# A 16-sublayer network on one core: conv's last normalisation in single blocks, a 64-byte scratch tile, and modulation portions from the eighth block on

## The chip, the cores and the metric

The kernel runs on one core of a Trainium2 chip as one launch. The metric is device time in microseconds (us) from start to end of an execution, lower is better. A profiled execution also gives a span, from the first instruction to the last, and a trace of every instruction. Engines: PE is TensorE (matrix products; PEld its weight loads), DVE is VectorE, ACT is ScalarE, POOL is GpSimd, SP is SyncE, which issues the loads here.

## What is computed

Three blocks follow one another on 256 tokens of width 1024: two layers each, with 16 sublayers in all. The change touches the conv sublayer of the first block, the masks of hgrn, and the feed-forwards in which the second block's modulation is prepared.

```python
def swiglu_ffn(x, w_in, w_out):
    gate, up = jnp.split(x @ w_in, 2, axis=-1)
    return (jax.nn.silu(gate) * up) @ w_out

def conformer_conv_module(x, w_in, b_in, w_dw, b_dw, ln_g, ln_b, w_out, b_out):
    a, gate = jnp.split(x @ w_in + b_in, 2, axis=-1)
    h = a * jax.nn.sigmoid(gate)
    h = lax.conv_general_dilated(h, w_dw[:, None, :], window_strides=(1,),
        padding=[(CONV_WIDTH - 1, 0)], ..., feature_group_count=D_MODEL) + b_dw
    h = jax.nn.silu(layer_norm(h, ln_g, ln_b))
    return h @ w_out + b_out

def second_block(...):
    cond = jax.nn.silu(c)
    for i in range(DEPTH):
        mod = cond @ ada_w[i] + ada_b[i]
        sh0, sc0, g0, sh1, sc1, g1, sh2, sc2, g2 = jnp.split(mod, N_MOD, axis=-1)
        h = modulate(rmsnorm(x, pre_norm[i, 0]), sh0, sc0)
        ...
```

## The kernel before

**Stages.** In order of time: f00, conv, f01, f10, hgrn, f11 (first block; f is a feed-forward), g00, dsa, g01, g10, diff, g11 (second; g is a modulated feed-forward), pool, m0, moba, m1 (third). conv lies at about 211 to 331 us, g00 at 1071 to 1246, g01 at 1363 to 1550.

**Weights.** Every weight matrix comes in chunks of 1 MB (`raw`, three buffers) through SP's queue, in order. ACT rounds a chunk to the matmul's fp32r type in four pieces (`hi`, L330), DVE forms the rest (`lo`, L334), and a product is made of three matmuls: hi by hi, lo by hi, hi by lo. There are five buffers of each, so these conversions run ahead of TensorE until the buffers are full.

**Order.** A scheduler sets the order of instructions on each engine from the order of the code and its dependences; buffers of a pool rotate by name. Each engine then runs its own list in order and waits by semaphores. `issue` (L624) lets code be written in at a given product of a sequence. `finish` (L657) does a sublayer's output product for token halves m = 0 and 1 and, ten products before the end of m = 1, has the next sublayer's transposes of the first half (`split_t`, L502) issued.

**Modulation portions.** The matrix of `ada_w` is worked off in portions of 128 outputs during feed-forwards that don't need it yet: a load of 512 KB (`adaw`, L1176, three buffers) and a multiply with a sum on DVE (`adaj`, L1186). f00, f01, f10 and f11 have 18 each, g00, g01 and g10 24 each, 144 in all. `more()` in `ffn` is called as weight chunks are taken, and does that share of the portions that has come due.

**conv.** Eight blocks of 128 channels: blocks 0 to 2 are convolved on DVE, blocks 3 to 7 on TensorE by `taps`, each in two parts of 16 matmuls on phase copies `ph` (L928). Results go to `y`; `mean` (L905), then the variance (`var`, L959) by one-column matmuls; `rest` (L956, L961) brings the last block's share; `r` is the reciprocal root by POOL, `rb` (L973) spreads it. Then `y` is normalised by groups of two blocks (L978, L979), SiLU on ACT (L983), rounded (L985) and its rest formed (L986). The output product starts with the bias (L990) and goes through L644.

**Scratch.** `prime` (L431) runs a one-column activation of a function that is needed soon, so that ACT loads its table early. Its tile is the first of the pool `tiny`.

Of the kernel before, what the change touches and what calls it, by code (L numbers as in the profile page):

```python
# [11 lines left out]
F32 = mybir.dt.float32  # L12
# [4 lines left out]
AF = mybir.ActivationFunctionType  # L17
# [4 lines left out]
S = 256  # L22
# [270 lines left out]
class _K:  # L293
# [137 lines left out]
    def prime(self, func, after):  # L431

        n = after.shape[0]
        t = self.tiny.tile([128, 1], F32, name="prime", bufs=1)
        self.nc.scalar.activation(t[:n], after, func, scale=0.0)

    def square(self, src, st, n):
# [286 lines left out]
    def ffn(self, s, act):  # L724
        nc, tc = self.nc, self.tc
        nf = 22
        with tc.tile_pool(name="hp_" + s, bufs=2) as hp:
            groups = {}
            jobs = self.ada_jobs.get(s, [])
            if jobs:  # L730
                self.ada_open(hp, jobs)
            takes = [0]

            def more():
                if jobs:
                    takes[0] += 1
                    with tc.issue_after(self.normed_last.ins):
                        self.ada_steps(min(len(jobs), -(-len(jobs) * takes[0] // 24)))

            def hidden(f, p):  # L740
                g, b = divmod(f, 2)
                if b == 0:
                    groups[g] = (hp.tile([128, 2, 256], F32R, name="hh", bufs=4), hp.tile([128, 2, 256], F32R, name="hl", bufs=4))
                hh, hl = groups[g]
                ragged = s[0] == "g" and f == nf - 1
                if ragged:

                    for t in (hh, hl):
                        nc.gpsimd.memset(t[64:, b].bitcast(F32), 0.0)
                n = 64 if ragged else 128  # L750
                sg = hp.tile([128, 256], F32, name="sg")
                h = hp.tile([128, 256], F32, name="h")
                self.added(sg[:n], p[0], slice(0, n))
                nc.scalar.activation(sg[:n], sg[:n], AF.Silu)
                self.added(h[:n], p[-1], slice(128 - n, 128))
                nc.vector.tensor_tensor(h[:n], sg[:n], h[:n], op=OP.mult)
                nc.scalar.activation(hh[:n, b], h[:n], AF.Copy)
                nc.vector.tensor_tensor(hl[:n, b], h[:n], hh[:n, b].bitcast(F32), op=OP.subtract)

            def hs(g):  # L760
                hh, hl = groups[g]
                return [(hh[:, b], hl[:, b]) for b in range(2)]

            p4 = self.first(s, ((0, 1), (2, 3)), act)
            hts = []
            for f in range(4):
                sg = hp.tile([128, 2, 128], F32, name="sg")
                if f % 2 == 0:
                    ht = hp.tile([128, 2, 2, 128], F32, name="hh" if f == 0 else "hl", bufs=4)
                h = ht[:, f % 2]  # L770
                for m in range(2):
                    pp = p4[f][m]
                    nc.scalar.activation(sg[:, m], pp[:, :128], AF.Silu)
                    nc.vector.tensor_tensor(h[:, m], sg[:, m], pp[:, 128:], op=OP.mult)
                hts.append(h)

            def turn():
                for g in range(2):
                    p = self.ps(("tr", "ps")[g])
                    for b in range(2):  # L780
                        for m in range(2):
                            nc.tensor.transpose(p[:, 256 * b + 128 * m:256 * b + 128 * m + 128], hts[2 * g + b][:, m], self.ident)
                    groups[g] = self.split(p, hp)

            self.rows_ahead(s)
            acc = None
            for g in range(2, 11):
                for f in (2 * g, 2 * g + 1):
                    w = self.take(("U", s, f))
                    if f > 4:  # L790
                        more()
                    p = [self.ps(t) for t in (("ps",) if s[0] == "g" and f == nf - 1 else ("ps", "tr"))]
                    products = self.wide_products(w, p)
                    if f == 4:
                        self.issue(products, 26, turn)
                    else:
                        self.issue(products)
                    hidden(f, p)
                    if f == 5:
                        acc = self.new_acc()  # L800
                    for j in ((0, 1) if f == 5 else (g - 1,) if f % 2 and g < 8 else ()):
                        w = self.take(("V", s, j))
                        more()
                        for m in range(2):
                            self.down(m, acc[m], w, hs(j), (128, 128), j == 0, False)
            if jobs:
                self.ada_close()
                self.rows_ahead(s, True)
            held = [(self.take(("V", s, g), g - 7), hs(g), (128, 128)) for g in (7, 8, 9, 10)]
            return self.finish(acc, held, self.cur_post)  # L810
# [58 lines left out]
    def conv(self, act):  # L869
        nc, tc = self.nc, self.tc  # L870
        with tc.tile_pool(name="cv", bufs=2) as cp:
# [18 lines left out]
            ones = cp.tile([128, 128], F32R, name="ones", bufs=1)  # L890
            nc.scalar.activation(ones, pick[:, :128], AF.Copy)
            bias = cp.tile([128, D], F32R, name="bias", bufs=1)
            nc.scalar.activation(bias, brow, AF.Copy)
            nc.vector.tensor_tensor(bias[32:33], brow[32:33], bias[32:33].bitcast(F32), op=OP.subtract)
            self.rows_ahead("conv")

            mean = self.ps("a2")
# [19 lines left out]
            for j in range(DVE_BLOCKS, 8):  # L917
# [5 lines left out]
                for i in range(2):  # L923
                    w = cp.tile([128, 16, 128], F32, name="taps", bufs=3)
                    nc.sync.dma_start(w.rearrange("p d c -> p (d c)"), self.a["ctaps"][2 * (j - DVE_BLOCKS) + i])
                    gv = g[64 * i:64 * i + 64].rearrange("p (t a) -> p a t", a=2)
                    for a in range(2):
                        nc.scalar.activation(x[64 * a:64 * a + 64, i, 15:], gv[:, a], AF.Copy)  # L928
                    for d in range(16):
                        nc.tensor.matmul(pc[:, i], lhsT=w[:, d], rhs=x[:, i, d:d + S // 2], start=(d == 0), stop=(d == 15))  # L930
                    yv = y[64 * i:64 * i + 64, j].rearrange("p (t a) -> p a t", a=2)
                    for a in range(2):
                        h = slice(64 * a, 64 * a + 64)
                        nc.scalar.activation(yv[:, a], pc[h, i], AF.Identity, bias=self.col("bph", 2 * j + i)[h])
                if j < 7:
                    summed(j)
                self.split_ahead(2)
                n = self.TAPS_BEHIND[j - DVE_BLOCKS]
                for at in left[:n]:
# [3 lines left out]
                left = left[n:]  # L943
            self.prime(AF.Silu, sg[:, :1])

            var = [self.ps("a3"), self.ps()]
            rest = self.ps("a0")
            for b in ((0, 1), (2, 3), (4, 5), (6,), (7,)):
                n = len(b)
                yb = y[:, b[0]:b[0] + n]  # L950
# [16 lines left out]
            nc.gpsimd.tensor_tensor(r, v, self.mhalf[:, :2], op=OP.pow)  # L967

            dg = cp.tile([128, 2, 128], F32, name="sg")
            rb = self.ps("a1")  # L970
            for m in range(2):
                nc.vector.tensor_scalar(dg[:, m], self.ident, r[:, m:m + 1], float(D), op0=OP.mult, op1=OP.mult)
                nc.tensor.matmul(rb[:, 128 * m:128 * m + 128], lhsT=means[:, 0], rhs=dg[:, m], start=True, stop=True)  # L973
            oact = self.new_act()
            for g in range(4):
                yg = y[:, 2 * g:2 * g + 2]
                for b in range(2):
                    nc.vector.tensor_tensor(yg[:, b], yg[:, b], rest[:, :S], op=OP.subtract)  # L978
                nc.vector.tensor_tensor(yg, yg, rb[:, None, :S].to_broadcast([128, 2, S]), op=OP.mult)  # L979
                z = cp.tile([128, 2, S], F32, name="sq")  # L980
                for b in range(2):
                    j = 2 * g + b
                    nc.scalar.activation(z[:, b], yg[:, b], AF.Silu, bias=self.col("lnb", j), scale=self.col("lng", j))  # L983
                h = oact[0][:, 2 * g:2 * g + 2]
                nc.scalar.activation(h, z, AF.Copy)  # L985
                nc.vector.tensor_tensor(oact[1][:, 2 * g:2 * g + 2], z, h.bitcast(F32), op=OP.subtract)  # L986
            acc = self.new_acc()
            for m in range(2):
                for n in range(2):
# [5 lines left out]
    def hgrn(self, act):  # L995
        nc, tc = self.nc, self.tc
        with tc.tile_pool(name="hg", bufs=2) as ho, ExitStack() as es:
# [75 lines left out]
            p4 = self.first("hgrn", _U_ORDER["hgrn"][:2], act)  # L1073
            mi = self.tmp.tile([128, D], I32, name="xn", bufs=1)
            nc.sync.dma_start(mi[:, :448], self.a["k_masks"])
            nc.vector.tensor_copy(masks.rearrange("p l t -> p (l t)"), mi[:, :448])
            self.rows_ahead("hgrn")
            for j in range(4):
                pf, pq = ([self.turned(p4[2 * j + i]) for i in range(2)] if j < 2 else
                          [self.proj_u(self.take(("U", "hgrn", 2 * j + i)), act) for i in range(2)])  # L1080
                vals = elems(j, pf, pq)
                for lev in range(8):
                    scores(j, *vals, lev)
            for n, s in enumerate(self.HALVES):
# [777 lines left out]
```

## Time and profile before

| | us |
|---|---|
| median of 3 runs | 2610.27 |
| lowest and highest | 2608.87, 2611.88 |
| profiled execution | 2617.61 |
| its span | 2615.1 |
| PE busy | 2570.5 (98%) |
| DVE busy | 1953.7 (75%) |
| ACT busy | 1504.6 (58%) |

The profiled execution is one of its own; its time lies 7.3 us above the median, so its rows are good for durations and waits, and differences are carried to the median. Its mean granted clock of TensorE is 0.995 of full speed.

### The profile page before, as it was taken

How to read it: one execution, taken by the hardware profiler on the slowest of the kernel's cores; microseconds unless marked ns; L12 is line 12 of the kernel's file. 1: busy time of each engine (PE TensorE's matmuls, PEld its weight loads, DVE VectorE, ACT ScalarE, POOL GpSimd, SP SyncE). 2: the span in 40 equal slices, each digit the busy share in tenths (PEclk: the TensorE clock that was granted, in tenths of full speed). 3: DMA queues.
4: the chain of work that ended last, by engine and by line, in shares of the span. 5: the costliest groups of instructions: out<-in, count | busy, mean ns of one | idle time of the engine just before them, and what ended most of it. 6: DMA issues, size and time to landing. Idle time of an engine off the chain costs nothing.

```text
span 2615.1 us, 37057 instructions
## 1 busy us (share of the span) xinstructions
PE 2570.5 (98%) x13302; PEld 2153.1 (82%) x13302; DVE 1953.7 (75%) x4175; ACT 1504.6 (58%) x3373; POOL 72.4 (3%) x158
## 2 busy tenths in 40 slices
PE   8999999999999999999999999999999999999999
PEld 7888888888888888888778888877788788877887
DVE  7868587687668886886969779777866866677664
ACT  5655455555644555655765565575655655566553
POOL 0000000000000000000000000000100000000000
PEclk9999899999999999999999999999999999999999
DMA  8847376486424675684448668653555545542552
GB/s 326 304 164 282 145 274 233 159 333 228 176 82 178 256 291 188 259 330 181 177 153 324 241 235 330 232 212 129 209 187 184 188 161 199 187 171 97 193 182 92
DMA packets 92711, 554.14 MB, mean 212 GB/s; under 512 B 10716, under 2 KB 11756, under 8 KB 38384
## 3 DMA queue, kind: packets, MB, share of 16 engines
q1 hardware_dynamic: 92528, 551.79, 57.3%
q8 instruction: 104, 1.70, 0.3%
q14 instruction: 79, 0.65, 0.1%
HBM read 550.62 MB, written 1.13 MB: 211 GB/s over the span
## 4 chain that ended last, share of the span: by engine, by line
PE 57%; issue 35%; ACT 3%; DVE 3%; DMA 1%; POOL 1%; SPq 0%; POOLq 0%; ACTq 0%; DVEq 0%
PE a L644 20%; PE ps L565 8%; PE tr L565 8%; PE ps L566 4%; PE tr L566 4%; PE a L603 2%; PE a L604 2%; PE a L605 2%; PE a L930 2%; DVE lo L334 1%; ACT hi L330 1%; PE tr L502 1%; DMA raw<-in_wall 1%; ACT junk L440 1%; POOL ry L446 1%
## 5 line engine op out<-in xcount | busy, mean ns | idle before, releaser
L334 DVE TENSOR_TENSOR lo<-raw,hi 128x512 fp32r<-128x512 f32 x1652 | 1062.5, 683 | 157.9 <-ACT hi L330 154.1
L330 ACT ACTIVATE hi<-raw 128x512 fp32r<-128x512 f32 x1652 | 926.9, 622 | 319.9 <-PE a L644 156.6
L565 PE MATMUL ps<-xh,hi 128*128 128x512 f32 x1344 | 489.1, 398 | 1.2 <-DVE sg L576 1.2
L565 PE MATMUL tr<-xh,hi 128*128 128x512 f32 x1312 | 477.5, 398 | 1.2 <-DVE ml L511 1.2
L566 PE MATMUL ps<-xh,lo 128*128 128x256 f32 x1344 | 349.9, 281 | 0.3 <-DVE lo L334 0.3
L566 PE MATMUL tr<-xh,lo 128*128 128x256 f32 x1312 | 341.9, 281 | 0.0
L644 PE MATMUL a<-hi,hh 128*128 128x512 f32 x960 | 309.5, 396 | 0.0
L644 PE MATMUL a<-hi,hl 128*128 128x512 f32 x960 | 309.3, 396 | 0.0
L644 PE MATMUL a<-lo,hh 128*128 128x512 f32 x960 | 308.9, 395 | 0.0
L565 PEld LDWEIGHTS ps<-xh,hi 128*128 128x128 f32 x1344 | 252.7, 188 | 51.3 <-DVE sg L576 1.9
L565 PEld LDWEIGHTS tr<-xh,hi 128*128 128x128 f32 x1312 | 247.7, 189 | 45.2 <-DVE ml L511 1.5
L566 PEld LDWEIGHTS ps<-xh,lo 128*128 128x128 f32 x1344 | 253.9, 189 | 15.9 <-DVE lo L334 0.5
L566 PEld LDWEIGHTS tr<-xh,lo 128*128 128x128 f32 x1312 | 248.1, 189 | 15.0
L644 PEld LDWEIGHTS a<-hi,hl 128*128 128x128 f32 x960 | 180.1, 188 | 43.4
L644 PEld LDWEIGHTS a<-lo,hh 128*128 128x128 f32 x960 | 180.1, 188 | 43.0
L644 PEld LDWEIGHTS a<-hi,hh 128*128 128x128 f32 x960 | 179.8, 188 | 40.1 <-ACT sg L832 0.2
L603 PE MATMUL a<-hi,xh 128*128 128x512 f32 x512 | 202.2, 396 | 3.1 <-ACT xh L510 1.9
L605 PE MATMUL a<-hi,xh 128*128 128x512 f32 x512 | 201.7, 395 | 0.0
L604 PE MATMUL a<-lo,xh 128*128 128x512 f32 x512 | 200.5, 392 | 0.2 <-DVE lo L334 0.2
L1186 DVE SCALAR_TENSOR_TENSOR adaj<-adaw,cond 128x1024 bf16<-128x1024 f32 x144 | 175.3, 1217 | 17.3 <-DMA adaw<-in_ada 17.0
L576 DVE TENSOR_TENSOR h<-h,tr 128x256 f32<-128x256 f32 x140 | 58.6, 419 | 150.7 <-ACT h L575 149.9
L575 ACT ACTIVATE h<-tr 128x256 f32<-128x256 f32 x140 | 53.6, 383 | 156.7 <-PE tr L565 156.6
(380 smaller groups left out, 3310.4 us busy)
## 6 DMA issues: line engine op xcount, KB each, us to landing
raw<-in_wall SPq DMA_DIRECT2D x413, 1024.0 KB, 4.8
adaw<-in_ada SPq DMA_DIRECT2D x144, 512.0 KB, 6.6
taps<-in_ctaps SPq DMA_DIRECT2D x10, 1024.0 KB, 7.4
G<-in_rows SPq DMA_DIRECT2D x16, 512.0 KB, 4.4
pg<-in_rows SPq DMA_DIRECT2D x12, 512.0 KB, 4.8
xn<-modd SPq DMA_DIRECT2D x12, 512.0 KB, 5.3
cond<-condd SPq DMA_DIRECT2D x7, 512.0 KB, 5.2
memt<-in_mem SPq DMA_DIRECT2D x4, 512.0 KB, 3.3
```

Of the source, the lines that this page charges most:

```text
L330: self.nc.scalar.activation(h[:, c], r[:, c], AF.Copy)
L334: self.nc.vector.tensor_tensor(l[:, c], r[:, c], h[:, c].bitcast(F32), op=OP.subtract)
L565: hi = lambda start, stop: mm(o, lhsT=wh[:, c], rhs=x.rearrange("p i t -> p (i t)"), start=start, stop=stop)
L566: lo = lambda: mm(o[:, :256], lhsT=wl[:, c], rhs=x[:, 0], start=False, stop=False)
L575: self.nc.scalar.activation(out, p[n, 256:], AF.Copy)
L576: self.nc.vector.tensor_tensor(out, out, p[n, :256], op=OP.add)
L603: yield self.nc.tensor.matmul(p, lhsT=xh[:, k, t], rhs=wh[:, c], start=(k == 0), stop=False)
L604: yield self.nc.tensor.matmul(p, lhsT=xh[:, k, t], rhs=wl[:, c], start=False, stop=False)
L605: yield self.nc.tensor.matmul(p, lhsT=xl[:, k, t], rhs=wh[:, c], start=False, stop=(k == 7))
L644: mm = lambda l, r, i, st, sp: nc.tensor.matmul(acc[i], lhsT=l[:k, t], rhs=r[:k, 1024 * b + 512 * i:1024 * b + 512 * i + 512], start=st, s ...
L930: nc.tensor.matmul(pc[:, i], lhsT=w[:, d], rhs=x[:, i, d:d + S // 2], start=(d == 0), stop=(d == 15))
L1186: self.nc.vector.scalar_tensor_tensor(junk, self.ada_w.pop(n), 1.0, self.cond, op0=OP.mult, op1=OP.mult, accum_out=self.mods[k][:, c:c + 1])
```

## The change

The change has four parts. `prime`'s tile grows from 4 to 64 bytes per partition, of which one column is used; with the allocator's steps of 32 bytes all later tiles move by 32 bytes. Conv's bias conversion and hgrn's mask conversion are written later in the code. Conv's last block and its normalisation are rewritten: two of the last four phase copies and one of the last bias additions go from ACT to DVE; `var`, `rest` and `rb` use the buffers `ps` and `tr` in place of the accumulators' `a0`, `a1`, `a3`; the normalisation goes by single blocks, with `z` in the buffers `gl`. In a feed-forward `more()` begins with the take of U block 7 (f > 6) rather than 5, V takes before that call no `more()`, and the share is counted by 20 rather than 24.

```diff
     def prime(self, func, after):
 
         n = after.shape[0]
-        t = self.tiny.tile([128, 1], F32, name="prime", bufs=1)
+
+        t = self.tiny.tile([128, 16], F32, name="prime", bufs=1)[:, :1]
...
-                        self.ada_steps(min(len(jobs), -(-len(jobs) * takes[0] // 24)))
+                        self.ada_steps(min(len(jobs), -(-len(jobs) * takes[0] // 20)))
...
-                    if f > 4:
+                    if f > 6:
                         more()
...
                         w = self.take(("V", s, j))
-                        more()
+                        if f > 5:
+                            more()
...
             bias = cp.tile([128, D], F32R, name="bias", bufs=1)
-            nc.scalar.activation(bias, brow, AF.Copy)
-            nc.vector.tensor_tensor(bias[32:33], brow[32:33], bias[32:33].bitcast(F32), op=OP.subtract)
             self.rows_ahead("conv")
...
                     for a in range(2):
-                        nc.scalar.activation(x[64 * a:64 * a + 64, i, 15:], gv[:, a], AF.Copy)
+                        if j == 7 and a == 1:
+                            nc.vector.tensor_copy(x[64 * a:64 * a + 64, i, 15:], gv[:, a])
+                        else:
+                            nc.scalar.activation(x[64 * a:64 * a + 64, i, 15:], gv[:, a], AF.Copy)
...
-                        nc.scalar.activation(yv[:, a], pc[h, i], AF.Identity, bias=self.col("bph", 2 * j + i)[h])
+                        bd = self.col("bph", 2 * j + i)[h]
+                        if j == 7 and i == a == 1:
+                            nc.vector.tensor_scalar(yv[:, a], pc[h, i], bd, None, op0=OP.add)
+                        else:
+                            nc.scalar.activation(yv[:, a], pc[h, i], AF.Identity, bias=bd)
                 if j < 7:
                     summed(j)
+                if j == 4:
+                    nc.scalar.activation(bias, brow, AF.Copy)
+                    nc.vector.tensor_tensor(bias[32:33], brow[32:33], bias[32:33].bitcast(F32), op=OP.subtract)
...
-            var = [self.ps("a3"), self.ps()]
-            rest = self.ps("a0")
+            var = [self.ps(), self.ps()]
+            rest = self.ps("tr")
...
-            rb = self.ps("a1")
+            rb = self.ps("tr")
...
-            for g in range(4):
-                yg = y[:, 2 * g:2 * g + 2]
-                for b in range(2):
-                    nc.vector.tensor_tensor(yg[:, b], yg[:, b], rest[:, :S], op=OP.subtract)
-                nc.vector.tensor_tensor(yg, yg, rb[:, None, :S].to_broadcast([128, 2, S]), op=OP.mult)
-                z = cp.tile([128, 2, S], F32, name="sq")
-                for b in range(2):
-                    j = 2 * g + b
-                    nc.scalar.activation(z[:, b], yg[:, b], AF.Silu, bias=self.col("lnb", j), scale=self.col("lng", j))
-                h = oact[0][:, 2 * g:2 * g + 2]
+            for j in range(8):
+                nc.vector.tensor_tensor(y[:, j], y[:, j], rest[:, :S], op=OP.subtract)
+                nc.vector.tensor_tensor(y[:, j], y[:, j], rb[:, :S], op=OP.mult)
+                z = cp.tile([128, S], F32, name="gl")
+                nc.scalar.activation(z, y[:, j], AF.Silu, bias=self.col("lnb", j), scale=self.col("lng", j))
+                h = oact[0][:, j]
                 nc.scalar.activation(h, z, AF.Copy)
-                nc.vector.tensor_tensor(oact[1][:, 2 * g:2 * g + 2], z, h.bitcast(F32), op=OP.subtract)
+                nc.vector.tensor_tensor(oact[1][:, j], z, h.bitcast(F32), op=OP.subtract)
...
             mi = self.tmp.tile([128, D], I32, name="xn", bufs=1)
             nc.sync.dma_start(mi[:, :448], self.a["k_masks"])
-            nc.vector.tensor_copy(masks.rearrange("p l t -> p (l t)"), mi[:, :448])
...
                 vals = elems(j, pf, pq)
+                if j == 0:
+                    nc.vector.tensor_copy(masks.rearrange("p l t -> p (l t)"), mi[:, :448])
```

In the changed kernel line numbers are one higher from `prime` on, and conv's are some six to ten higher: the bias product L990 is L996 there, the taps L930 are L933, the variance L959 is L969, `rb` L973 is L983, the output product L644 is L645, the portion's multiply L1186 is L1193 and L774 is L775.

On TensorE, from the end of conv's statistics to its output product, before (`a_2916` and `a_2917` belong to the second token half, `a_2914` and `a_2915` to the first):

```order
L959 MATMUL ps<-means,sq 128x1
L990 MATMUL a_2916<-bias,ones 128x512
L990 MATMUL a_2917<-bias,ones 128x512
L973 MATMUL a_2877<-sg,means 128x128 x2
L644 MATMUL a_2916<-hi,xh 128x512
L644 MATMUL a_2917<-hi,xh 128x512
...
L644 MATMUL a_2916<-hi,xh 128x512
L990 MATMUL a_2914<-bias,ones 128x512
L644 MATMUL a_2914<-hi,xh 128x512
```

The same place in the changed kernel, from the end of the mean on (`a_2930` and `a_2931` belong to the first token half):

```order
L905 MATMUL a_2135<-y,means 128x256
L996 MATMUL a_2930<-bias,ones 128x512
L996 MATMUL a_2933<-bias,ones 128x512
L933 MATMUL a_2767<-ph_1952,taps 128x128 x16
L969 MATMUL ps<-means,sq 128x1 x8
L933 MATMUL a_2767<-ph_1952,taps 128x128 x16
L969 MATMUL ps<-means,sq 128x1 x6
L996 MATMUL a_2931<-bias,ones 128x512
L966 MATMUL tr<-means,y 128x1 x2
L971 MATMUL tr<-y,means 128x256
L969 MATMUL ps<-means,sq 128x1 x2
L996 MATMUL a_2932<-bias,ones 128x512
L983 MATMUL tr<-sg,means 128x128 x2
L645 MATMUL a_2930<-hi,xh 128x512
```

Two bias products have moved ahead of the last taps and two among the statistics. Before, 13 products of the second half are followed by the first half's 48 and then by the other 35 of the second; after, all 48 of the first half come ahead of all 48 of the second.

On DVE, early in g00, before (`adaj` is a portion, `hl` of L774 the gated product of hidden blocks 2 and 3, L576 the read that frees a result buffer):

```order
L334 TENSOR_TENSOR lo<-raw,hi 128x512 x4
L774 TENSOR_TENSOR hl<-sg,a_10076 128x128
L334 TENSOR_TENSOR lo<-raw,hi 128x512
L1186 SCALAR_TENSOR_TENSOR adaj,mods_102<-adaw,cond 128x1024
L774 TENSOR_TENSOR hl<-sg,a_10076 128x128
...
L576 TENSOR_TENSOR sg<-sg,ps 128x256
L1186 SCALAR_TENSOR_TENSOR adaj,mods_102<-adaw,cond 128x1024
```

The same place in the changed kernel:

```order
L775 TENSOR_TENSOR hl<-sg,a_10092 128x128
L334 TENSOR_TENSOR lo<-raw,hi 128x512 x2
L775 TENSOR_TENSOR hl<-sg,a_10092 128x128
...
L577 TENSOR_TENSOR sg<-sg,ps 128x256
L334 TENSOR_TENSOR lo<-raw,hi 128x512 x3
L1193 SCALAR_TENSOR_TENSOR adaj,mods_102<-adaw,cond 128x1024
L721 TENSOR_TENSOR hl<-tr,hh 128x512
```

The first portion has moved behind both `hl` and the first `sg`. In SP's queue, early in g01, two loads of `adaw` now follow five of `raw`, where before each of the first two followed one to three. The bias and mask conversions stand between the same neighbours on ACT and DVE as before.

## Rows read from the trace of the kernel before

**Rows 1.** Busy time, share of the span and instructions (the page's first part)

```profile
PE 2570.5 (98%) x13302; PEld 2153.1 (82%) x13302; DVE 1953.7 (75%) x4175; ACT 1504.6 (58%) x3373; POOL 72.4 (3%) x158
```

**Rows 2.** Timeline of conv's tail: start, us, engine, line, operation, [idle before <- releaser]

```profile
287.48 1.32 ACT L928 ACTIVATE ph<-gl 64x128 f32<-64x128 f32 x4
...
288.18 5.47 PE L930 MATMUL a<-ph,taps 128*128 128x128 f32 x32 [2.25 <-ACT ph L928]
...
293.48 0.28 PE L959 MATMUL a<-means,sq 128*128 128x1 f32 x2
...
295.19 3.82 PE L930 MATMUL a<-ph,taps 128*128 128x128 f32 x32
...
298.84 0.28 PE L959 MATMUL a<-means,sq 128*128 128x1 f32 x2
```

**Rows 3.** TensorE in 2-us windows: length, busy (instructions), granted clock, DMA share, GB/s

```profile
290.00:292.00 2.00, 2.00 (x11) 0.50 0.24 53
...
304.00:306.00 2.00, 0.48 (x3) 0.50 0.00 0
...
310.00:312.00 2.00, 2.00 (x6) 0.50 0.00 0
```

**Rows 4.** A gap of TensorE in the stage dsa, and its clock behind it

```profile
1274.45 0.47 PE L1422 MATMUL tr<-ident,dup 128*128 128x128 f32 x2 [1.65 <-DVE dup L1421]
...
1276.00:1278.00 2.00, 1.95 (x9) 1.00 0.88 369
```

**Rows 5.** Timeline of conv's normalisation and output product

```profile
300.34 0.42 ACT L953 ACTIVATE sq<-y 128x256 f32<-128x256 f32 x1 [0.55 <-DVE y L951]
...
304.52 0.69 DVE L979 TENSOR_TENSOR y<-y,a 128x512 f32<-128x512 f32 x1 [0.52 <-PE a L973]
...
305.24 1.09 ACT L983 ACTIVATE sq<-y,cols 128x256 f32<-128x256 f32 x2 [3.52 <-DVE y L979]
...
306.37 0.63 ACT L985 ACTIVATE xh<-sq 128x512 fp32r<-128x512 f32 x1
306.38 0.41 DVE L978 TENSOR_TENSOR y<-y,a 128x256 f32<-128x256 f32 x1
...
307.05 1.22 PE L644 MATMUL a<-hi,xh 128*128 128x512 f32 x2 [2.57 <-ACT xh L985]
...
308.92 1.91 PE L644 MATMUL a<-hi,xh 128*128 128x512 f32 x4
```

**Rows 6.** Timeline, end of conv's output product and the next stage's transposes

```profile
324.51 0.60 ACT L440 ACTIVATE junk<-a 128x512 bf16<-128x512 f32 x1 [0.67 <-PE a L644]
...
326.35 1.07 PE L644 MATMUL a<-hi,xh 128*128 128x512 f32 x4
...
330.85 1.32 PE L502 MATMUL tr<-ident,xn 128*128 128x128 f32 x8 [0.71 <-DVE xn L487]
```

**Rows 7.** Timeline near the start of the feed-forwards g00 and g01

```profile
1090.23 1.22 DVE L1186 SCALAR_TENSOR_TENSOR adaj<-adaw,cond 128x1024 bf16<-128x1024 f32 x1 [1.93 <-DMA adaw<-in_ada]
...
1091.71 0.33 PE L782 MATMUL ps<-ident,hl 128*128 128x128 f32 x1 [1.17 <-DVE hl L774]
...
1383.41 1.22 DVE L1186 SCALAR_TENSOR_TENSOR adaj<-adaw,cond 128x1024 bf16<-128x1024 f32 x1
...
1385.02 0.50 PE L565 MATMUL ps<-xh,hi 128*128 128x512 f32 x1 [0.96 <-DVE sg L576]
```

**Rows 8.** Waits: engine, line waited for, total us, times, longest us

```profile
PE ps L565 <- DVE sg L576: 1.2, 2, 1.0
...
DVE adaj L1186 <- DMA adaw<-in_ada: 17.0, 17, 2.5
```

**Rows 9.** Groups of ACT's exponentials in dsa, then in diff

```profile
L1348 ACT ACTIVATE e<-e,mx 128x256 f32<-128x256 f32 x16 | 7.9, 494 | 0.0
...
L1348 ACT ACTIVATE e<-e,mx 128x256 f32<-128x256 f32 x16 | 7.9, 496 | 0.0
```

**Rows 10.** DMA issues: count, KB each, median us to landing (the page's sixth part)

```profile
adaw<-in_ada SPq DMA_DIRECT2D x144, 512.0 KB, 6.6
```

## Prediction

> **What bounds the kernel now.** I read the page's busy times first: TensorE (PE) is busy for 2570.5 of 2615.1 us, 98% of the span [rows 1]. A change can therefore only win in two ways: close one of TensorE's few gaps, or let its instructions run at the higher clock. So I went next through the list of its waits and through timelines of the places that the change touches, and read the granted clock there in 2-us windows. Four findings carry the sum.
>
> First, conv's tail. TensorE stands still for 2.25 us until ScalarE (ACT) has copied the last phases (`ph`, L928), then runs the last taps [rows 2]. A microsecond later its granted clock is 0.50, the 1.2 GHz level [rows 3]: the first 32 taps need 5.30 us to the next instruction (288.18 to 293.48), the second 32, at full clock, 3.65 us (295.19 to 298.84) [rows 2]. A gap of 1.65 us in dsa was not followed by such a fall: the clock there stayed at 1.00 [rows 4].
>
> Second, the normalisation. From the first multiply by the standard deviation's inverse (L979, 304.52) to the first output product (L644, 307.05) TensorE waits for a chain of single instructions on blocks taken in pairs; the clock falls again here and is still 0.50 in the window that begins at 310 [rows 3, 5].
>
> Third, the transposes of the next stage's first half (L502) come 0.71 us late, because only 25 output matmuls lie between the end of the first token half and them, while the chain of square, reciprocal root and scaling takes 330.85 - 324.51 = 6.34 us [rows 6].
>
> Fourth, early in the feed-forwards g00 and g01 a modulation portion on VectorE (DVE, L1186, 1.22 us) waits for its load or stands ahead of an instruction that TensorE needs: 1.17 us lost at 1091.71 and 0.96 at 1385.02 [rows 7].
>
> **The change part by part, against the profiled execution (2617.61 us).**
>
> *Conv's last block.* Two of four phase copies go to DVE; ACT's four take 1.32 us together, 0.33 each [rows 2]. Before, taps can start when two copies are done on ACT. After, ACT does one while DVE does the other; DVE has a weight piece in front of it, so I give this 0.2 us. Two bias matmuls move into the gap. Four matmuls of this shape take 1.07 us [rows 6], so two are worth 0.5 us of the gap filled, and the standstill shrinks from 2.25 to some 2.25 - 0.2 - 0.5 = 1.55 us. This is under the 1.65 that left the clock alone in dsa [rows 4]. I therefore take the fall as avoided: 5.30 - 3.65 = 1.65 us. It could also be nothing, if the clock falls all the same. Together -1.85, between -0.2 and -1.9.
>
> *Statistics.* The order shows that the variance products keep their number. The other two bias matmuls move into the short waits here, +0.2 us where they don't fit, against some 0.3 of idle that they fill: -0.1. The squares and the reciprocal root stay as they are.
>
> *Single blocks.* The first multiply shrinks from 128x512 (0.69) to 128x256 (0.41), the first rounding copy from 0.63 to 0.42; the two SiLUs of the pair take 1.09 [rows 5]. ACT's order after the change still has two SiLUs ahead of the first copy, so the 0.55 of the second stays in the chain, and I count 0.28 + 0.21 = -0.49 (-1.0 if the copy came at once). What follows the first block: per block DVE needs three passes of 0.41 (1.23 us), ACT 0.55 + 0.42 = 0.97; before, a pair cost DVE 0.82 + 2 x 0.69 = 2.20 and ACT 1.72. So splitting costs (2 x 1.23 - 2.20) x 4 = 1.04 us on DVE and (2 x 0.97 - 1.72) x 4 = 0.88 on ACT. This is covered by TensorE, which uses six matmuls per block: 1.6 us at the full clock, 2.9 at the half (four take 1.07 or 1.91 [rows 5, 6]). If that cover were gone, the 1.04 would be paid.
>
> *Bias and half order.* The bias matmuls no longer stand in the output phase: two there cost between 0.53 (full) and 0.95 (half clock); I take 0.6. Freed accumulators let the first token half's 48 products run at once and then the second's 48, so 38 instead of 25 stand between the first half's end and L502. 25 took 6.34 - 0.71 = 5.63 us, so 38 take 8.6 us [rows 6], more than the chain of 6.34: the 0.71 goes, and with the restart behind it some 0.9. Together -1.5; at least -0.9.
>
> *Modulation portions.* They start at the eighth block instead of the fifth, and the order shows DVE with no L1186 ahead of g00's `hl` (L774) and g01's `sg` (L576). In g00 the wait of 1.17 should vanish. In g01 a second wait of the same kind, with no portion ahead of it, cost the 0.2 that is left of the line's 1.2 less 1.0 [rows 8]; so I take -0.7 of 0.96. Sum -1.9, between -1.2 and -2.1. No portion is dropped: the same 144 loads and multiplies come slightly later, and their total on an engine that is busy 75% of the time [rows 1] stays.
>
> *Offset and conversions.* The wider `prime` shifts all later tiles by 32 bytes. Rows that price such a shift: the same exponentials in dsa, where tiles lie at multiples of 64 bytes, and in diff, where they lie at odd multiples of 32, take 494 and 496 ns [rows 9]. That is nothing. The moved bias and mask conversions stand between the same neighbours in the engines' orders as before: nothing.
>
> Sum: -1.85 - 0.1 - 0.49 - 1.5 - 1.9 = **-5.8 us**; bounds -2.8 (no clock gain, smallest terms) and -6.8. The profiled execution would take 2611.8. It is 7.3 us above the median of the runs (2610.27), so I carry the difference over, not the level, and shave 0.3 because a clock fall need not occur in every execution: 2610.27 - 5.5 = **2604.8 us**.
>
> **Rivals.** About 0.2%, 5.2 us, is what a measurement of this kernel can tell from no change, and the forecast lies only just past it.
>
> *Small pieces bind the tail.* If DVE or ACT, not TensorE, sets the pace of the eight blocks, the 1.04 us come onto the path, and about as much again because weight pieces (L334) share DVE: +2 us, 2606.8, within 0.2%. For it: 1.23 per block is close to TensorE's 1.6. Against: the half clock makes TensorE slower there, not faster. The Trainium skill, "VectorE: DVE Perf Modes", section on the TRN2 errata, speaks against this edit: it says that an SBUF-sourced instruction pays a fixed extra latency, and advises tiles of 512 elements or more. By that rule the split could only lose; the trace agrees on the fixed part (0.41 and 0.69 are not in the ratio of 256 to 512 [rows 5]), but the first result comes sooner with the smaller piece.
>
> *The clock falls all the same.* Then 1.65 us are missing: 2606.4, within 0.2%. For it: 1.55 is an estimate a tenth of a microsecond below the one gap known to be harmless. Against: bias matmuls sit inside the gap.
>
> *Slower: late portions.* In the order, SP's queue issues up to five weight chunks ahead of the portions' loads in g01 where before it was three. A portion's load takes 6.6 us to land [rows 10], and DVE already waits 17 times for one, up to 2.5 us [rows 8]. In the new place the waiting multiply stands ahead of L576 and L334, which free PSUM and feed TensorE, and denser portions (20 steps instead of 24) leave less slack. Each such stall that reaches TensorE costs up to 2.5. It decides from 5.8 + 5.2 = 11 us, that is five stalls of the longest kind, 12.5 us; that gives 2610.27 - 5.8 + 12.5 = 2617.0. Against: the 17 waits now reach TensorE only twice [rows 7].
>
> *The change doesn't do what it says.* Moved conversions stay where they were (above), and if the offset is what matters, its price is in no row here; one per mille of DVE's 1953.7 us [rows 1] would be 2 us either way. Left at 2604.8 plus or minus 2.
>
> **How the numbers follow.** Forecast as summed 0.48, of it nearly all beyond 5.2 us; small pieces 0.15; the clock falls 0.2; offset or partly failed portions that leave 2 to 5 us 0.08; late portions and other losses 0.09, of which a part still ends within 0.2%. So faster 0.48, same 0.44, slower 0.08. The range reaches from 2600.5 (all upper bounds, and some luck with the second half-clock stretch) to 2611.0 (the terms cancelled by one stall or two).
>
> **What would show each step.** Right: the tail's L928 gap under 1.7 us and a clock of 1.00 in the windows behind it; 32 taps in 3.7 us; L644 starting some 0.5 us sooner after the first multiply; no wait of L502 for `xn` at the end of conv; no wait of L782 in g00. Wrong: a clock of 0.50 still behind the first tail gap, L644's first pass waiting for `xh` block by block, new waits for `adaw` ahead of L576 in g00, g01 or g10, or the same lines' mean durations changed by the offset across the whole kernel.

## The result, and the profile after

The changed kernel takes 2595.36 us (2593.93 to 2599.25, 4 runs); the kernel before, beside it, 2611.07 (2608.87 to 2611.99). The ratio is 0.9943, 95% interval [0.9926, 0.9961]: 15 us or 0.6% faster. The forecast was 2604.8 with a range from 2600.5 to 2611.0, so the direction was right and the size was not: nearly three times the 5.5 us that were summed.

The profiled execution took 2596.23 us, with a span of 2594.5. Its first line has the shares of [rows 1] to within one point; PE's busy time is 21.8 us shorter, with the same 13302 instructions:

```profile
PE 2548.7 (98%) x13302; PEld 2148.0 (83%) x13302; DVE 1952.7 (75%) x4186; ACT 1502.0 (58%) x3374; POOL 72.1 (3%) x158
```

**Conv's tail** came as forecast. In the timeline the gap ahead of the last taps is 1.62 us instead of 2.25 [rows 2], and the first 32 taps take 3.65 us to the next instruction (287.55 to 291.20) instead of 5.30. From the first multiply to the first output product it is 1.90 us (301.62 to 303.52), against 2.53 in [rows 5]. The next stage's transposes have no wait behind them where [rows 6] had 0.71:

```profile
287.02 0.65 ACT L931 ACTIVATE ph<-gl 64x128 f32<-64x128 f32 x2
...
287.55 3.81 PE L933 MATMUL a<-ph,taps 128*128 128x128 f32 x32 [1.62 <-ACT ph L931]
...
291.20 1.84 PE L969 MATMUL ps<-means,sq 128*128 128x1 f32 x16
...
301.62 1.08 DVE L987 TENSOR_TENSOR y<-y,tr 128x256 f32<-128x256 f32 x3
...
303.52 1.22 PE L645 MATMUL a<-hi,xh 128*128 128x512 f32 x2 [1.94 <-ACT xh L991]
...
325.37 1.03 PE L503 MATMUL tr<-ident,xn 128*128 128x128 f32 x8
```

In windows of 2 us (length, busy, granted clock), the clock stays at 1.00 behind the first gap. It falls behind the second as in [rows 3], and is back at 1.00 by 310:

```profile
290.00:292.00 2.00, 2.00 (x21) 1.00 0.57 156
...
304.00:306.00 2.00, 2.00 (x6) 0.50 0.00 0
...
310.00:312.00 2.00, 2.00 (x11) 1.00 0.28 74
```

**Where the rest came from.** When the two traces are laid side by side instruction by instruction, the changed one runs ahead by a little more in every feed-forward, all the way to m1 at the end, where nothing was edited: some 0.3 to 0.5 us in each 40 us. In the attention stages, which have no hidden tiles, it gains nothing of the kind. The next place to look was therefore a stretch of m1 in which TensorE does only output products of hidden tiles (`hh`, `hl`). The timeline of the kernel before, two products to a row, has a new row each 0.46 to 0.47 us:

```profile
2592.07 0.63 PE L644 MATMUL a<-lo,hh 128*128 128x512 f32 x2
2592.54 0.63 PE L644 MATMUL a<-hi,hl 128*128 128x512 f32 x2
2593.00 0.63 PE L644 MATMUL a<-hi,hh 128*128 128x512 f32 x2
```

In the changed kernel, in the same stretch, there is one each 0.45 to 0.46 us:

```profile
2572.00 0.61 PE L645 MATMUL a<-lo,hh 128*128 128x512 f32 x2
2572.45 0.62 PE L645 MATMUL a<-hi,hl 128*128 128x512 f32 x2
2572.91 0.62 PE L645 MATMUL a<-hi,hh 128*128 128x512 f32 x2
```

The granted clock is 1.00 in both (20 us of TensorE, with the number of products that it got through; before, then after):

```profile
2590.00:2610.00 20.00, 20.00 (x87) 1.00 0.07 26
```

```profile
2570.00:2590.00 20.00, 20.00 (x90) 1.00 0.07 26
```

Over all 2,880 such products the mean from start to start (leaving out gaps over 0.4 us) is 233.8 ns before and 227.9 after (counted in the two traces): 2,880 x 5.9 ns = 17 us. What moved is their stationary operand: with the 64-byte scratch tile, hidden tiles lie 32 bytes further, while the weights (`hi`, `lo`) and `xh` stay, since they are allocated ahead of it.

### The profile page after: what moved, and what is told of

It is laid out like the page before. It is cut to its first block, busy times and chain, and to the rows that moved or that the text cites. A ratio compares the mean times of both kernels' runs of the same rounds, so it can differ in the third digit from the quotient of the medians.

```text
span 2594.5 us, 37086 instructions
## 1 busy us (share of the span) xinstructions
PE 2548.7 (98%) x13302; PEld 2148.0 (83%) x13302; DVE 1952.7 (75%) x4186; ACT 1502.0 (58%) x3374; POOL 72.1 (3%) x158
## 4 chain that ended last, share of the span: by engine, by line
PE 58%; issue 32%; DVE 4%; ACT 3%; DMA 2%; POOL 1%; SPq 0%; POOLq 0%; ACTq 0%; DVEq 0%
PE a L645 21%; PE tr L566 8%; PE ps L566 8%; PE tr L567 4%; PE ps L567 4%; PE a L604 2%; PE a L605 2%; PE a L606 2%; DMA raw<-in_wall 2%; PE a L933 1%; DVE lo L334 1%; ACT hi L330 1%; PE a L1380 1%; PE tr L503 1%; PE a L1337 1%
## 5 line engine op out<-in xcount | busy, mean ns | idle before, releaser
L566 PE MATMUL ps<-xh,hi 128*128 128x512 f32 x1344 | 489.0, 398 | 0.0
L566 PE MATMUL tr<-xh,hi 128*128 128x512 f32 x1312 | 477.9, 398 | 1.8 <-DVE ml L512 1.2
L645 PE MATMUL a<-hi,hh 128*128 128x512 f32 x960 | 304.8, 391 | 0.0
L645 PE MATMUL a<-hi,hl 128*128 128x512 f32 x960 | 303.4, 390 | 0.0
L645 PE MATMUL a<-lo,hh 128*128 128x512 f32 x960 | 303.1, 390 | 0.0
L566 PEld LDWEIGHTS ps<-xh,hi 128*128 128x128 f32 x1344 | 252.6, 188 | 49.1
L566 PEld LDWEIGHTS tr<-xh,hi 128*128 128x128 f32 x1312 | 247.6, 189 | 46.4 <-DVE ml L512 1.5
L645 PEld LDWEIGHTS a<-lo,hh 128*128 128x128 f32 x960 | 180.2, 188 | 37.7
L645 PEld LDWEIGHTS a<-hi,hl 128*128 128x128 f32 x960 | 180.2, 188 | 37.2
L645 PEld LDWEIGHTS a<-hi,hh 128*128 128x128 f32 x960 | 179.9, 188 | 35.4 <-ACT sg L834 0.2
L604 PE MATMUL a<-hi,xh 128*128 128x512 f32 x512 | 201.4, 394 | 3.9 <-ACT xh L516 2.1
L1193 DVE SCALAR_TENSOR_TENSOR adaj<-adaw,cond 128x1024 bf16<-128x1024 f32 x144 | 175.5, 1219 | 33.1 <-DMA adaw<-in_ada 32.5
L605 PE MATMUL a<-lo,xh 128*128 128x512 f32 x512 | 199.8, 391 | 0.2 <-DVE lo L334 0.2
L577 DVE TENSOR_TENSOR h<-h,tr 128x256 f32<-128x256 f32 x140 | 58.5, 418 | 138.1 <-ACT h L576 137.5
L576 ACT ACTIVATE h<-tr 128x256 f32<-128x256 f32 x140 | 53.4, 381 | 138.2 <-PE tr L566 138.2
```

What stands on the lines that cost most here:

```text
L566: hi = lambda start, stop: mm(o, lhsT=wh[:, c], rhs=x.rearrange("p i t -> p (i t)"), start=start, stop=stop)
L576: self.nc.scalar.activation(out, p[n, 256:], AF.Copy)
L577: self.nc.vector.tensor_tensor(out, out, p[n, :256], op=OP.add)
L604: yield self.nc.tensor.matmul(p, lhsT=xh[:, k, t], rhs=wh[:, c], start=(k == 0), stop=False)
L605: yield self.nc.tensor.matmul(p, lhsT=xh[:, k, t], rhs=wl[:, c], start=False, stop=False)
L645: mm = lambda l, r, i, st, sp: nc.tensor.matmul(acc[i], lhsT=l[:k, t], rhs=r[:k, 1024 * b + 512 * i:1024 * b + 512 * i + 512], start=st, s ...
```

## The experiments

Theory P says that this placement brings nearly all of the gain; theory T, the prediction's, that the tail and the portions do, and the offset nothing. The first four kernels take the change apart, in runs beside each other.

**The offset alone.**

```diff
-        t = self.tiny.tile([128, 1], F32, name="prime", bufs=1)
+        t = self.tiny.tile([128, 16], F32, name="prime", bufs=1)[:, :1]
```

> The kernel before with the 64-byte scratch tile alone. Theory P (operand placement: the 2,880 output products whose stationary operand is a hidden tile go from 234 to 227 ns each because stage tiles and weight tiles now lie alike): 16 to 19 us faster, about 2593 to 2595, with the 227 ns in every feed-forward. Theory T (the tail and the portions bring the gain, the offset nothing, as predicted): within 2 us of before.

2597.46 us, ratio 0.9942 [0.9930, 0.9954], or -15 us; hidden products take 227.9 ns in the trace. P holds, T falls.

**All but the offset.** The changed kernel with the old tile:

```diff
-        t = self.tiny.tile([128, 16], F32, name="prime", bufs=1)[:, :1]
+        t = self.tiny.tile([128, 1], F32, name="prime", bufs=1)
```

> The changed kernel with the old 4-byte scratch tile. Theory P: the 234 ns come back and 16 to 19 us with them, so the time is 2611 to 2614, no faster than before. Theory T: 2595, the gain stays. If the predicted terms for tail and portions hold beside P: 2605.

2608.77 us, ratio 0.9985 [0.9977, 0.9994], or -3.9 us; hidden products 233.9 ns again. P's statement that nothing would be left was too strong: tail and portions are worth some 4 us. The interval, -6.0 to -1.6, also holds the -5.5 that the prediction summed for them.

**Conv's tail alone** (the kernel before with the diff's lines in `conv`):

```diff
+                        if j == 7 and a == 1:
+                            nc.vector.tensor_copy(x[64 * a:64 * a + 64, i, 15:], gv[:, a])
...
+            var = [self.ps(), self.ps()]
+            rest = self.ps("tr")
...
+            for j in range(8):
```

> The kernel before with conv's new last block and single-block normalisation alone. Predicted terms: -3.9 us, with the first clock fall gone and L502 of the next stage not waiting. Rival (the gain is given back in the next stage's start): -1 to 0 us.

2611.64 us, ratio 0.9988 [0.9979, 0.9997], or -3.1 us, with -3.9 inside the interval. The trace shows the tail's steps as in the changed kernel: the clock is 1.00 from 288 to 294, and L502 doesn't wait.

**The portions alone.**

```diff
-                        self.ada_steps(min(len(jobs), -(-len(jobs) * takes[0] // 24)))
+                        self.ada_steps(min(len(jobs), -(-len(jobs) * takes[0] // 20)))
...
-                    if f > 4:
+                    if f > 6:
...
-                        more()
+                        if f > 5:
+                            more()
```

> The kernel before with the later modulation portions alone. Predicted terms: -1.9 us, no wait of L782 in g00. Rival (loads come late behind the weights, waits for adaw grow as the changed kernel's 22 waits of 32.5 us suggest): 0 to +4 us.

2613.52 us, ratio 0.9999 [0.9989, 1.0009]: no gain that these runs can tell. The timeline of g00 shows one of the two waits still there. There is no portion ahead of `hl` any more, but `hl` now waits 2.34 us for ACT's `sg`, and TensorE as long as before (1.24 against 1.17 in [rows 7]):

```profile
1083.71 0.25 ACT L773 ACTIVATE sg<-a 128x128 f32<-128x128 f32 x1
...
1084.00 0.29 DVE L774 TENSOR_TENSOR hl<-sg,a 128x128 f32<-128x128 f32 x1 [2.34 <-ACT sg L773]
...
1084.34 0.33 PE L782 MATMUL ps<-ident,hl 128*128 128x128 f32 x1 [1.24 <-DVE hl L774]
```

In the trace of before, `sg` came sooner after TensorE's stop: the stop was at 1090.55 there (1083.10 here), and `sg` ended at 1090.72 (1083.96 here). The portion then held `hl` until 1091.38:

```profile
1090.46 0.26 ACT L773 ACTIVATE sg<-a 128x128 f32<-128x128 f32 x1
```

Portions do come later, as the rival said, and DVE waits longer for them: its total grew from the 17.0 of [rows 8] to 32.5 us in the changed kernel. TensorE loses little by it: in the feed-forwards of the portions-only trace, two waits on DVE's `hl` (L720) are new, 0.5 us in sum, one of them right behind a portion.

```profile
DVE adaj L1193 <- DMA adaw<-in_ada: 32.5, 22, 3.3
```

**Which placement?** The next runs move tiles only. Addresses here are those of the built programs; before, hidden tiles lie at 192 and weights and `xh` at 224, modulo 512. Theory S says that the stationary operand's own place decides, theories E64 to E512 that the two operands of a product have to lie alike modulo that many bytes.

Weights and all behind them 32 bytes on:

```diff
         self.rope2 = self.cst.tile([128, 2, 2, 16], F32, name="rope2")
+        self.nc.gpsimd.memset(self.cst.tile([128, 8], F32, name="pad"), 0.0)
```

> The kernel before with 32 bytes put ahead of the weight tiles, so that weights lie at 0 and hidden tiles at 96 (addresses modulo 128; before 96 and 64); one small memset more. Theory E64 (the two operands of a product have to lie alike modulo 64): unlike, 234 ns, time as before, 2610 to 2614. Theory S (the stationary operand has to lie at an odd multiple of 32): 227 ns, 15 us faster, about 2597.

2612.52 us, ratio 0.9995 [0.9985, 1.0006]; 233.8 ns. The hidden tiles lie where the changed kernel has them (224), the weights don't. S falls, E64 stands.

The same and the 64-byte scratch tile:

```diff
+        self.nc.gpsimd.memset(self.cst.tile([128, 8], F32, name="pad"), 0.0)
...
+        t = self.tiny.tile([128, 16], F32, name="prime", bufs=1)[:, :1]
```

> As the one with weights moved, and the 64-byte scratch tile as well: weights at 0, hidden tiles at 0 modulo 128. E64, and E128 (alike modulo 128): 227 ns, 15 us faster, about 2597. S: 234 ns, as before.

2596.94 us, ratio 0.9930 [0.9913, 0.9947]; 228.0 ns. Alike again, at another place, and as fast.

A scratch tile of 128 bytes:

```diff
+        t = self.tiny.tile([128, 32], F32, name="prime", bufs=1)[:, :1]
```

> The kernel before with a scratch tile of 128 bytes: weights at 96, hidden tiles at 32 modulo 128, so alike modulo 64 and not modulo 128. E64 and S: 227 ns, 15 us faster, about 2597. E128: 234 ns, as before.

2610.38 us, ratio 0.9983 [0.9971, 0.9995]; 234.1 ns: alike modulo 64 is not enough. The 4 us that it did gain come from elsewhere (last section).

A scratch tile of 192 bytes:

```diff
+        t = self.tiny.tile([128, 48], F32, name="prime", bufs=1)[:, :1]
```

> The kernel before with a scratch tile of 192 bytes: hidden tiles 160 bytes further than before, alike with the weights modulo 128 (96 and 96) and unlike modulo 256. Theory E128: 227 ns for the hidden products, 15 us faster, about 2597. Theory E256 (alike modulo 256 or more is needed): 233 to 234 ns, as before, 2610 to 2614.

2610.41 us, ratio 0.9991 [0.9980, 1.0002]; 233.4 ns: alike modulo 128 is not enough either. E128 falls.

The changed kernel with 256 bytes ahead of `xh`, so that `xh` and hidden tiles are alike with the weights modulo 256 but not modulo 512:

```diff
+            self.nc.gpsimd.memset(self.act.tile([128, 64], F32, name="pad"), 0.0)
             self.both = self.act.tile([128, 8, 2, 256], F32R, name="xh")
```

> The changed kernel with 256 bytes put ahead of xh, so that xh and the hidden tiles both lie alike with the weights modulo 256 and unlike modulo 512. Theory E256: hidden and xh products stay at 227 ns, time as the changed kernel, 2593 to 2597. Theory E512 (alike modulo 512 is needed): both kinds rise to 229 to 234 ns, 15 to 30 us slower than the changed kernel, L565's products perhaps 3 us less in sum.

2593.10 us, ratio 0.9927 [0.9905, 0.9949]; hidden products 227.9 ns, `xh` products as before. E256 holds, E512 falls.

**Does it hold for other products?** The kernel before with 32 bytes ahead of `xh`: hidden tiles become alike with the weights, `xh` unlike.

```diff
+            self.nc.gpsimd.memset(self.act.tile([128, 8], F32, name="pad"), 0.0)
             self.both = self.act.tile([128, 8, 2, 256], F32R, name="xh")
```

> The kernel before with 32 bytes put ahead of the activations' tile xh alone: weights stay at 96 modulo 128, xh goes from 96 to 0, hidden tiles behind it from 64 to 96. Theory E128: the 2,880 hidden products fall to 227 ns (-15 to -18 us), and the some 2,600 products of xh with weights that took 227 ns rise to 233 or 234 (+16 us); L565 and L566, unlike now too, rise by up to as much each. In sum 2610 to 2640. Theory H (only the hidden tiles' own place matters): 15 us faster, about 2597, xh products at 227.

2600.50 us, ratio 0.9955 [0.9940, 0.9971], or -12 us. Mean distances in ns, before and here:

| stationary, moving | count | before | here | us |
|---|---|---|---|---|
| `hh` or `hl`, weights (L644) | 2,880 | 233.8 | 228.7 | -14.7 |
| `xh`, weights (L603 and L605) | 1,408 | 231.4 | 236.9 | +7.8 |
| `xh`, weights (L604) | 704 | 230.1 | 234.8 | +3.3 |
| `xh`, weights (L644) | 480 | 234.8 | 239.3 | +2.2 |
| weights, `xh` (L565) | 2,656 | 235.5 | 231.8 | -9.9 |
| weights, first half of `xh` (L566) | 2,656 | 117.3 | 118.0 | +1.9 |

The rows add up to -9.4 us of the 12. Another 1.6 us may be the clock's: in this trace it didn't fall behind conv's first gap (next section). Hidden and `xh` products went the two ways that E128, and E256 too, foresee; H, by which `xh` would stay, falls. But the time lies outside the 2610 to 2640 of E128, because L565, where the weights are stationary, got faster by being unlike: there the rule fails.

The other products of 128x512 whose stationary tile lies behind the scratch tile go along with the hidden ones: 192 on `mh`, `ml`, `ov` and `oscT` take 234.6 ns before and 228.6 in the changed kernel.

**Does the rest add?** Offset and tail together, without the portions and with the mask conversion at its old place:

```diff
+        t = self.tiny.tile([128, 16], F32, name="prime", bufs=1)[:, :1]
...
+            for j in range(8):
```

> Offset and conv's tail together, portions and mask conversion as before. If the two add: -15.2 - 3.1 = -18 us, about 2594, as fast as the changed kernel or a little faster. If the portions matter beside them: 2 us or more apart from the changed kernel's 2595.

2595.13 us, ratio 0.9924 [0.9909, 0.9940], or -20 us: no slower than the changed kernel, so beside the other two parts no gain of the portions can be seen.

**Pairs again in the changed kernel's normalisation:**

```diff
-            for j in range(8):
+            for g in range(4):
+                yg = y[:, 2 * g:2 * g + 2]
```

> The changed kernel with the normalisation by pairs of blocks again, the rest of its tail kept. Predicted term: the first output product 0.5 us later, so +0.5 us. Rule of the larger pieces: 1 to 2 us faster with pairs, the splitting's 1.04 us of DVE no longer on the path.

2592.58 us, ratio 0.9925 [0.9907, 0.9943], whose interval overlaps the changed kernel's. The time thus bears out neither the +0.5 us nor the rule of the larger pieces. The timeline separates the step: from the first multiply to the first output product it is 2.52 us here, and 1.90 in all five traces with single blocks. At the next stage the two traces are 0.8 us further apart than ahead of the normalisation, in favour of single blocks; but traces of one tail differ by as much there, so the 0.62 of the chain is shown and its price in time is not.

```profile
302.38 0.69 DVE L989 TENSOR_TENSOR y<-y,tr 128x512 f32<-128x512 f32 x1
...
304.90 1.22 PE L645 MATMUL a<-hi,xh 128*128 128x512 f32 x2 [2.57 <-ACT xh L995]
```

Three kernels (offset with tail, pairs, 256 bytes) have medians below the changed kernel's, by 0.2 to 2.8 us; their intervals overlap with its own, so none is shown to beat it.

## Why the prediction was wrong

**The step that failed** is the one on the offset: "That is nothing." It took its price from two groups of ACT instructions [rows 9], that is from one engine's own reads at two absolute places. The offset acts on TensorE, where it made 2,880 products 5.9 ns faster each, and it acts by where a product's two operands lie relative to each other. No row of ACT or DVE could have shown it. It cost 15 us of the forecast, and of the rival that named the offset: "2 us either way" was taken from DVE's time, the wrong engine's. The sum of the other terms is not contradicted: without the offset the change is worth 3.9 us, 1.6 to 6.0, where 5.5 were summed. With these 3.9 us alone the time would lie inside the forecast's range.

The trace of before did have a sign of it, which the prediction passed by. Products of the same shape run at two distances there: four L644 products of `xh` take 1.07 us [rows 6], a median of 227 ns from start to start, and those of hidden tiles 234, at the same clock. 7 ns on 2,880 instructions of the engine that is busy 98% of the time is more than all the gaps that the sum closed. The prediction had listed waits, and a slower instruction waits for nothing.

**Conv's last block and the clock**: right on the gap (-0.63 us; 1.62 or 1.63 in all six traces with the new tail), and right on the clock, but its price is not paid in every execution. The clock is 1.00 behind the shorter gap in all six. Behind the old gap of 2.25 us it fell in six traces of eight; in the other two (128-byte scratch tile, 32 bytes ahead of `xh`) it stayed:

```profile
288.79 3.84 PE L931 MATMUL a<-ph,taps 128*128 128x128 f32 x32 [2.25 <-ACT ph L929]
...
290.00:292.00 2.00, 2.00 (x20) 1.00 0.14 16
```

So the 1.65 us are won only where the clock would have fallen, and a gap of this length doesn't decide that alone. The 0.3 us that the forecast took off for this had no row behind it; two of eight would give 1.65 / 4 = 0.4.

**Statistics**: right. From the first variance product behind the last taps to `rb` it is 4.31 us (296.56 to 300.87), before 4.45 (298.84 [rows 2] to 303.29). `rb`'s own four products took 0.71 us instead of 1.19, since they still ran at the full clock's pace. This was not in the sum, and is luck: in two of the six traces with the new tail they took 1.12 and 1.22.

```profile
303.29 1.19 PE L973 MATMUL a<-sg,means 128*128 128x128 f32 x4 [0.83 <-DVE sg L972]
```

```profile
296.56 1.40 PE L969 MATMUL ps<-means,sq 128*128 128x1 f32 x12
...
300.87 0.71 PE L983 MATMUL tr<-sg,means 128*128 128x128 f32 x4 [1.01 <-DVE sg L982]
```

**Single blocks**: right on the first product, and somewhat more than its -0.49 (0.62). The rule of larger pieces, from the Trainium skill, "VectorE: DVE Perf Modes", section on the TRN2 errata, did not decide here: behind the first product TensorE waits for no block in the changed kernel's timeline, so the added 1 us is covered, as the step said, and the shorter head of the chain counts.

**Bias and half order**: right, L503 waits no more. All of the tail: -3.94 forecast, -3.1 [-5.5, -0.8] measured. From the same instruction ahead of the gap (before at 279 us) to the same one in the next stage (342 us) it is 61.3 to 63.3 us in the eight traces with the old tail and 58.5 to 59.6 in the five with the new one and single blocks; the means differ by 3.7.

**Portions**: not borne out. -1.9 was forecast; -0.3 [-2.9, +2.4] was measured, which excludes neither nothing nor the forecast. The traces show what was wrong: the step took two waits of one trace for fixed prices. The g00 wait (1.17 in [rows 7]) is there with the late portions too, 0.5 in the changed kernel and 1.2 with the portions alone, and gone in the three others. With the old portions it is gone in four traces of nine, and 0.4, 0.9, 1.2, 1.2 and 2.1 in the rest. g01's wait (0.96) is 0 to 0.6 in the other eight with the old portions and 0 to 0.5 with the late ones. Where `sg` was ready, the portion did hold `hl`, by 0.66 us in the trace of before (1090.72 to 1091.38); the rest of that 1.17 was `sg` itself. What makes `sg` late in one execution and not in another is open.

**Conversions**: they didn't move in the engines' orders, and no run here tries them alone; tail and portions alone add to -3.4 us, all but the offset to -3.9.

## What to carry to other kernels

When a kernel is bound by one engine, compare the distance from start to start of like instructions on that engine, between tiles and between stages, before listing waits: a few nanoseconds on thousands of instructions outweigh any gap. An edit that moves addresses has to be costed on every engine that reads the moved tiles, with both operands' places. And a wait or a fall of the clock that stands in one trace is a fixed price only if it stands in several: here a wait of 1.17 us and a loss of 1.65 us came and went between traces of the same code in that place.

## What the runs showed of the hardware

A stream of 128x512 fp32r products whose stationary operand is an activation (`hh`, `hl`, `xh`) and whose moving operand is a weight tile runs at a median of 227 ns from start to start when both tiles start alike modulo 256 bytes (differences 0 and 256). At differences of 32 (either way), 64 and 128 the medians are 232 to 235 ns. No others were tried. Why is open. The load of the next product's stationary tile overlaps the running product, and the next tile lies like the present one, so no run tells which of the two meets the moving tile. The Trainium skill, "TensorE: Matmul & The Clock Gate", section "Step-by-step: what each phase is for", says that TensorE has two independent read ports, so that loading the next weights takes nothing from the running product; a difference by relative place is not what one expects from that, and the measurement decides.

With the roles turned (weights stationary, `xh` moving, L565, alternating with the shorter L566) a difference of 32 made it faster, 231.8 against 235.5 ns, and 256 changed nothing (235.6). And in the kernel with the 128-byte scratch tile L565 took 234.4 ns, though neither its weights nor `xh` had moved: 2,656 x 1.1 ns = 2.9 us, the greater part of that kernel's 4 us. Both are unexplained. Tiles that other engines read and write meanwhile had moved, so a clash with those is a rival that no run here tests, for L565 at least.
